# Where the Strassen weight sums of an MLP are issued: ACT and GpSimd during the front, or GpSimd alone during front, merge and MLP

## The chip, the cores and the metric

The kernel runs on one core of a Trainium2 chip. The metric is device time in microseconds from launch to the last output; lower is better. The kernel before took 915.79 us (median of three runs, 911.35 to 919.47).

## What is computed

One layer of a hybrid encoder over 528 tokens (16 learned ones and 512 of the input), width 1024:

```python
u = rmsnorm(h, norm_mix)
proj = u @ w_in                                  # RWKV features, FoX features, gates
y_rw = rwkv7_branch(proj[..., :C_RW], ...)       # 8 heads, delta rule over the sequence
y_fx = fox_branch(proj[..., C_RW:C_RW + C_FX], ...)  # 8 heads, forgetting attention
merged = sig(g_A) * (y_rw @ w_out_rw) + sig(g_B) * (y_fx @ w_out_fx)
h = h + merged @ w_o
z = rmsnorm(h, norm_mlp)
h = h + square(relu(z @ w_up)) @ w_down          # 1024 -> 4096 -> 1024
```

Everything is float32. Large products are made in three passes of a split of each operand into a high and a low part.

## The kernel before

The program has three stages.

**The front** (`tile_trunk_kernel`, lines 271 to 1033). u is held in SBUF as a high and a low part. 24 projection blocks feed the recurrent heads and the attention heads, 16 more make the gates, which go to DRAM (`gd`). Several streams (the chain over chunks, the recurrent pairs, attention, FoX features, weight sums, projections) are written as generators, and `Turns.run` (line 166) lets them take turns: a stream gives back the time at which it wants to go on, and a small planner, `Clock`, keeps a model time. The order of TensorE's instructions is the order in which the streams emit them; the other engines' order is made by a scheduler. Weights are loaded by SyncE in halves of 128x512 (256 KB, tile `wraw`, four buffers), cast to the high part by ACT (`whi`) and subtracted to the low part (`wlo`), in the front by GpSimd (line 450), elsewhere by VectorE (line 237).

**The merge** (lines 1048 to 1134). Eight blocks m: two halves of `w_out`, two gates read back from DRAM (`gl0`, `gl1`, two buffers each), tanh on ACT, 24 matmuls, two multiplications on VectorE (line 1068), one addition of the two branches on GpSimd (line 1070), then `mhi` (ACT, 1071) and `mlo` (VectorE, 1072). Early up weights are loaded and split in between (1084 to 1090). Then the product with `w_o`, its first half from `load_w` (1094), its second from eight loads into `wohi` and `wolo` (1099 to 1102), the residual, the norm and the transposes to `zhi` and `zlo`.

**MLP** (lines 1138 to 1288). The hidden width is cut into three slices of 4, 6 and 6 pairs of 256 columns (`SLICES`). In each slice the up product makes a pair's squared relu `R` out of two blocks, and `left_factors` makes seven left factors of it; then seven products per pair (a Strassen-Winograd form of the down product) run against seven right factors. Three of these are quarters of `w_down`; four are sums of quarters, T1 to T4, held in DRAM as `tsum`, in eight pieces of 256x512 (512 KB) each, one for two pairs. A product's weights are loaded as they are needed, two ahead.

**The weight sums** (lines 1001 to 1026) are made by DMA from DRAM to DRAM. For each of the eight pieces there are four copies and four additions (`accum_op=add`):

```python
t1 = b11; t1 += b12      t3 = b12; t3 += b22
t2 = b22; t2 += t1       t4 = b21; t4 += t2
```

That is 64 transfers. The stream `weight_sums` emits them at rank -1, the n-th at model time 45 + 6 n us: copies go to ACT's queue, additions to GpSimd's, each tied behind the last instruction of its engine so that the scheduler cannot move it ahead. A copy is emitted two steps ahead of its addition. All 64 are issued in the front.

Of the kernel before, what the change touches and what calls it, by code (L numbers as in the profile page):

```python
# [9 lines left out]
F32 = mybir.dt.float32  # L10
# [4 lines left out]
ALU = mybir.AluOpType  # L15
# [12 lines left out]
CDEC = math.exp(-0.5)  # L28
SLICES = (4, 6, 6)
FIRST = (0, 4, 10)  # L30


C_MU = 0
# [155 lines left out]
def kernel(ctx, tc, ht, x, win, par, cst, gain, lora, wout, wo, wup, wdn, out, dbg=None):  # L189
    nc = tc.nc  # L190
# [76 lines left out]
    gates_d = [dr.tile([128, S], F32, name=f"gd{i}") for i in range(16)]  # L267
    quarters = [[wdn[i][256 * c:256 * c + 256] for c in range(8)] for i in range(4)]
    tsum = [[dr.tile([256, 512], F32, name=f"tsum{i}") for c in range(8)] for i in range(4)]

    with ExitStack() as st:
        up = st.enter_context(tc.tile_pool(name="up", bufs=1))
# [726 lines left out]
        turns.add(2, attention())  # L999
        turns.add(3, fox_features())  # L1000
        def weight_sums():

            def part(t, c):
                return t[c].rearrange("(a b) c -> a (b c)", b=2)

            def behind(dma, engine):
                x = next(x for x in reversed(nc.cur_bb.bb.instructions) if str(x.engine).endswith(engine) and x.name != dma.ins.name)
                tc.add_manual_dep(dma.ins, x.name, mybir.DependencyInfo(mybir.DependencyClass.NoSync, mybir.DependencyReason.DATA),
                                  reason="spread over the front")

            t1, t2, t3, t4 = tsum
            b11, b12, b22, b21 = quarters
            steps = []
            for c in range(8):
                for a, b in (((t1, b11), (t1, b12)), ((t3, b12), (t3, b22)), ((t2, b22), (t2, t1)), ((t4, b21), (t4, t2))):
                    steps += [(*a, c, False), (*b, c, True)]
            for n in range(1, len(steps) - 2, 2):
                steps[n], steps[n + 1] = steps[n + 1], steps[n]
            for n, (dst, src, c, adds) in enumerate(steps):
                yield lambda: 45.0 + 6.0 * n  # L1020
                if adds:
                    behind(nc.gpsimd.dma_start(part(dst, c), part(src, c), accum_op=ALU.add, max_dma_last_dim=2048), "Pool")
                else:
                    behind(nc.scalar.dma_start(part(dst, c), part(src, c), max_dma_last_dim=2048), "Activation")

        turns.add(-1, weight_sums())
        turns.add(8, projections(24 + 16))
# [20 lines left out]
    with ExitStack() as st:  # L1048
        mp = st.enter_context(tc.tile_pool(name="mp", bufs=1))
        for j, src in enumerate((y_rw, y_fx)):  # L1050
            for k in range(4):
                split(yhi[:, 4 * j + k, :], ylo[:, 4 * j + k, :], src[:, k, :])
        mhi = mp.tile([128, KB, S], F32R, name="mhi")
        mlo = mp.tile([128, KB, S], F32R, name="mlo")
        for m in range(KB):
            w = load_w(wout[m])
            pp = []
            for br in range(2):
                g = mp.tile([128, S], F32, name=f"gl{br}", bufs=2)
                nc.sync.dma_start(g, gates_d[8 * br + m])  # L1060
                act(g, g, AF.Tanh, scale=0.5)
                po = ppo()
                n = 0
                for k in range(4 * br, 4 * br + 4):
                    for a, b in passes(wk(w, k), (yhi, ylo)):
                        mm(po, a, b[:, k, :], start=n == 0, stop=n == 11)  # L1066
                        n += 1
                V.scalar_tensor_tensor(g, g, 1.0, po, ALU.add, ALU.mult)
                pp.append(g)
            G.tensor_tensor(pp[0], pp[0], pp[1], ALU.add)  # L1070
            merged = act(mhi[:, m, :], pp[0], AF.Copy, scale=0.5)
            V.scalar_tensor_tensor(mlo[:, m, :], pp[0], 0.5, mhi[:, m, :].bitcast(F32), ALU.mult, ALU.subtract)
        M = (mhi, mlo)
        wohi = mp.tile([128, KB, 512], F32R, name="wohi")
        wolo = mp.tile([128, KB, 512], F32R, name="wolo")
        gB = mp.tile([128, 1024], F32, name="gB2")
        nc.sync.dma_start(gB, gain.to_broadcast([128, 1024]))
        for i in range(4):
            nc.sync.dma_start(hres[:, i, :], x[128 * i:128 * i + 128, :])
        zhi = hp.tile([128, KB, S], F32R, name="zhi", tag="zhi")  # L1080
        zlo = hp.tile([128, KB, S], F32R, name="zlo", tag="zlo")
        pin = pinned(merged)
        early = []
        for j in range(2):
            we = yp.tile([128, 2, 2, 512], F32R, name=f"we{j}", tag=("y_rw", "y_fx")[j])
            for x in range(2):
                raw = wp.tile([128, 512], F32, name="wraw", bufs=4)
                nc.sync.dma_start(raw, wup[j][:, 512 * x:512 * x + 512])
                split(we[:, x, 0, :], we[:, x, 1, :], raw)
            early.append([(we[:, x, 0, :], we[:, x, 1, :]) for x in range(2)])  # L1090

        pd = [ppo() for i in range(4)]
        for b2 in range(4):
            w = load_w(wo[0, b2])
            for i, b1 in [(i, b1) for b1 in range(2) for i in range(4)] if b2 < 3 else [(i, b1) for i in range(4) for b1 in range(2)]:
                k = 2 * b2 + b1
                for n, (a, b) in enumerate(passes(M, w[b1])):
                    mm(pd[i], a[:, k, 128 * i:128 * i + 128], b, start=k == 0 and n == 0, stop=k == 7 and n == 2)
        for k in range(KB):
            raw = wp.tile([128, 512], F32, name="wraw", bufs=4)  # L1100
            nc.sync.dma_start(raw, wo[1, k // 2][:, 512 * (k % 2):512 * (k % 2) + 512])
            split(wohi[:, k, :], wolo[:, k, :], raw)
        ssb = mp.tile([128, 4], F32, name="ssb")
        for i in range(4):
            hr = hres[:, i, :512]
            V.tensor_tensor(hr, hr, pd[i], ALU.add)
            xt = mp.tile([128, 1024], F32, name="xt2", bufs=2)
            act(xt[:, :512], hr, AF.Square, accum_out=ssb[:, i:i + 1])
            V.tensor_scalar(ssb[:, i:i + 1], ssb[:, i:i + 1], 1.0 / 1024, 1e-6, ALU.mult, ALU.add)
        for i in range(4):  # L1110
            po = ppo()
            n = 0
            for k in range(KB):
                for a, b in passes(M, (wohi, wolo)):
                    mm(po, a[:, k, 128 * i:128 * i + 128], b[:, k, :], start=n == 0, stop=n == 23)  # L1115
                    n += 1
            hr = hres[:, i, :]
            V.tensor_tensor(hr[:, 512:], hr[:, 512:], po, ALU.add)
            xt = mp.tile([128, 1024], F32, name="xt2", bufs=2)
            ss = mp.tile([128, 1], F32, name="ss2", bufs=2)  # L1120
            act(xt[:, 512:], hr[:, 512:], AF.Square, accum_out=ss)
            a_ = act(ss, ss, AF.Ln, bias=ssb[:, i:i + 1], scale=1.0 / 1024)
            after(a_, pin)
            act(ss, ss, AF.Exp, scale=-0.5)
            tk = slice(128 * i, 128 * i + 128)
            for j in range(2):
                cols, kk = slice(512 * j, 512 * j + 512), slice(4 * j, 4 * j + 4)
                V.scalar_tensor_tensor(xt[:, cols], hr[:, cols], ss, gB[:, cols], ALU.mult, ALU.mult)
                pt = ppd().rearrange("p (b c) -> p b c", c=128)
                for k in range(4):  # L1130
                    nc.tensor.transpose(pt[:, k, :], xt[:, 512 * j + 128 * k:512 * j + 128 * k + 128], ident)
                A.copy(zhi[:, kk, tk], pt)
                V.tensor_tensor(zlo[:, kk, tk], pt, zhi[:, kk, tk].bitcast(F32), ALU.subtract)
        dump("hres", hres.rearrange("p a b -> p (a b)"))
# [3 lines left out]
    with ExitStack() as st:  # L1138
# [43 lines left out]
        x6, x7 = ([ppd() for i in range(2)] for _ in range(2))  # L1182

        later = []

        def soon(*jobs):
            later.extend(jobs)

        for p0, n_pairs in zip(FIRST, SLICES):
# [10 lines left out]
            for n, b_ in enumerate(blocks):  # L1200
                if held:
                    w, po = held.pop(0)
                    up_part(w, po, 256, 512)
                else:
                    w = load_w(wup[b_])
                    po = ppo()
                    up_part(w, po, 0, 512)
                if n == 2 * n_pairs - 1:
                    fill(AHEAD)
                if n % 2 == 0:  # L1210
                    R = yp.tile([128, 8, 256], F32, name="R", tag=("y_rw", "y_fx")[n // 2 % 2])
                    up_evac(po, R[:, 0:8:7, :])
                else:
                    up_evac(po, R[:, 1:3, :])
                    left_factors(fhi, flo, n // 2, R)

            first, last = p0 == 0, p0 + n_pairs == 16
# [148 lines left out]
```

## Time and profile before

| | |
|---|---|
| median of three runs | 915.79 us |
| profiled execution | 918.31 us, span 916.5 us |
| TensorE busy | 860.8 us (94%) |
| VectorE, ACT, GpSimd busy | 601.1, 464.6, 187.7 us |
| mean DMA rate | 141 GB/s, 129.46 MB in 69772 packets |
| weight load of the front | 256 KB, 3.2 us from issue to landing |
| copy of a sum (ACT's queue) | 512 KB, 4.4 us |
| addition of a sum (GpSimd's queue) | 512 KB, 7.4 us from `w_down`, 6.7 us from another sum |

A row of the table of windows gives the length of a stretch, the busy time of TensorE, its weight loads, VectorE, ACT and GpSimd (with the count of instructions), the granted TensorE clock, the busy share of the 16 DMA engines and GB/s. A row of the chain of waits gives start, length, engine and what was done or waited for; the chain is followed back from the last instruction. A row of the time line gives start, length, engine, line, operation, and in brackets the idle time of the engine just before it with what ended it. A row of waits gives who waited for whom: total us, times, longest. In the list of DMA issues stand the queue, the count, the size and the median time to landing. Register, branch and DMA-issuing instructions are not counted as busy.

### The profile page before, as it was taken

The page shows a single profiled execution, that of the slowest core. Times are in us where ns is not written, and L with a number is a line of the kernel's source. Part 1 is how long each engine was busy: PE and PEld are TensorE (multiplying, and loading weights), DVE is VectorE, ACT ScalarE, POOL GpSimd, SP SyncE. Part 2 cuts the span into 40 slices and gives each one's busy share as a digit, 9 for nine tenths or more (in the row PEclk, how much of TensorE's full clock was granted, in tenths as well). Part 3 has the DMA queues.
Part 4 walks back from the last instruction along what each step waited for, and adds up shares of the span by engine and source line. Part 5 has one row for each costly group of instructions (what it writes and reads, how often), then busy time and mean ns, then how long its engine had stood idle before and what let it go on. Part 6 is the DMA issues. An engine that isn't in the chain of part 4 may idle for free.

```text
span 916.5 us, 15714 instructions
## 1 busy us (share of the span) xinstructions
PE 860.8 (94%) x5868; PEld 699.9 (76%) x5868; DVE 601.1 (66%) x1174; ACT 464.6 (51%) x939; POOL 187.7 (20%) x177
## 2 busy tenths in 40 slices
PE   6589897999989899999999999999999999999998
PEld 4587785867887777767867877888888888888886
DVE  7966875555877697465366756467556675566776
ACT  7756342585545443467364645245544454344542
POOL 4253533314533345222401210000000000000000
PEclk9889988999989899999997999999999999999999
DMA  6122634748464546665686644024632356422465
GB/s 209 46 71 70 161 94 136 185 105 209 105 140 117 138 133 188 174 161 138 152 218 218 213 164 128 1 79 131 193 126 93 104 178 194 156 96 101 137 222 170
DMA packets 69772, 129.46 MB, mean 141 GB/s; under 512 B 6840, under 2 KB 7992, under 8 KB 69696
## 3 DMA queue, kind: packets, MB, share of 16 engines
q1 hardware_dynamic: 52288, 94.91, 32.0%
q0 software_dynamic: 8704, 16.78, 11.4%
q10 hardware_dynamic: 8704, 16.78, 5.5%
q8 instruction: 46, 0.75, 0.3%
q14 instruction: 30, 0.25, 0.1%
HBM read 122.13 MB, written 39.86 MB: 177 GB/s over the span
## 4 chain that ended last, share of the span: by engine, by line
PE 72%; DVE 16%; DMA 4%; ACT 4%; issue 3%; POOL 0%; POOLq 0%; SPq 0%; ACTq 0%; DVEq 0%
PE po L1145 19%; PE pj L478 17%; PE po L1235 12%; PE pd L1235 5%; PE po L1066 2%; PE po L1115 2%; DMA wraw<-in_win 2%; PE pw L830 2%; PE py L627 1%; PE psc L582 1%; DVE tmp L812 1%; DVE AX L824 1%; PE pbt L778 1%; DVE xt L379 1%; PE psr L763 1%
## 5 line engine op out<-in xcount | busy, mean ns | idle before, releaser
L237 DVE TENSOR_TENSOR wlo<-wraw,whi 128x512 fp32r<-128x512 f32 x196 | 138.3, 713 | 95.4 <-ACT whi L236 95.3
L236 ACT CAST whi<-wraw 128x512 fp32r<-128x512 f32 x200 | 123.7, 621 | 134.8 <-PE po L1145 43.9
L478 PE MATMUL pj<-uhi,whi 128*128 128x264 f32 (+1 forms) x480 | 170.9, 356 | 10.4 <-ACT gt L489 4.7
L478 PE MATMUL pj<-uhi,wlo 128*128 128x264 f32 (+1 forms) x480 | 158.5, 330 | 0.0
L478 PE MATMUL pj<-ulo,whi 128*128 128x264 f32 (+1 forms) x480 | 158.4, 330 | 0.0
L450 POOL TENSOR_TENSOR wlo<-wraw,whi 128x512 fp32r<-128x512 f32 x80 | 110.3, 1389 | 173.9 <-ACT whi L449 155.4
L478 PEld LDWEIGHTS pj<-uhi,whi 128*128 128x128 f32 x480 | 94.3, 197 | 31.9 <-issue 11.6
L478 PEld LDWEIGHTS pj<-uhi,wlo 128*128 128x128 f32 x480 | 94.7, 197 | 7.2
L478 PEld LDWEIGHTS pj<-ulo,whi 128*128 128x128 f32 x480 | 95.0, 198 | 4.2
L1145 PE MATMUL po<-zhi,whi 128*128 128x512 f32 (+1 forms) x248 | 94.8, 382 | 0.0
L1145 PE MATMUL po<-zlo,whi 128*128 128x512 f32 (+1 forms) x248 | 94.8, 382 | 0.0
L1145 PE MATMUL po<-zhi,wlo 128*128 128x512 f32 (+1 forms) x248 | 94.8, 382 | 0.0
L449 ACT CAST whi<-wraw 128x512 fp32r<-128x512 f32 x80 | 49.4, 618 | 52.4 <-PE pj L478 29.8
L1235 PE MATMUL po<-wlo,fhi 128*128 128x512 f32 x160 | 62.3, 390 | 0.0
L1235 PE MATMUL po<-whi,flo 128*128 128x512 f32 x160 | 62.3, 390 | 0.0
L1235 PE MATMUL po<-whi,fhi 128*128 128x512 f32 x160 | 62.2, 389 | 0.0
L1145 PEld LDWEIGHTS po<-zlo,whi 128*128 128x128 f32 x248 | 46.6, 188 | 9.1
L1145 PEld LDWEIGHTS po<-zhi,wlo 128*128 128x128 f32 x248 | 46.6, 188 | 9.0
L1145 PEld LDWEIGHTS po<-zhi,whi 128*128 128x128 f32 x248 | 46.6, 188 | 9.0
L1157 ACT CAST fhi<-R 128x768 fp32r<-128x768 f32 (+1 forms) x32 | 30.2, 944 | 24.2 <-DVE R L1164 13.6
L1158 DVE TENSOR_TENSOR flo<-R,fhi 128x768 fp32r<-128x768 f32 (+1 forms) x32 | 34.8, 1088 | 7.8 <-ACT fhi L1157 7.8
L1235 PEld LDWEIGHTS po<-wlo,fhi 128*128 128x128 f32 x160 | 30.0, 188 | 6.5 <-DVE wlo L237 0.2
(295 smaller groups left out, 1667.9 us busy)
## 6 DMA issues: line engine op xcount, KB each, us to landing
wraw<-in_win SPq DMA_DIRECT2D x84, 256.0 KB, 3.2
tsum<-in_wdn ACTq DMA_DIRECT2D x32, 512.0 KB, 4.4
wraw<-in_wup SPq DMA_DIRECT2D x64, 256.0 KB, 2.6
wraw<-tsum SPq DMA_DIRECT2D x64, 256.0 KB, 2.8
wraw<-in_wdn SPq DMA_DIRECT2D x48, 256.0 KB, 2.6
tsum<-in_wdn POOLq DMA_DIRECT2D x16, 512.0 KB, 7.4
tsum<-tsum POOLq DMA_DIRECT2D x16, 512.0 KB, 6.7
gd<-gt SPq DMA_DIRECT2D x16, 256.0 KB, 2.4
```

Of the source, the lines that this page charges most:

```text
L236: A.copy(hi, raw)
L237: low.tensor_tensor(lo, raw, hi.bitcast(F32), ALU.subtract)
L449: A.copy(hi, raw)
L450: G.tensor_tensor(lo, raw, hi.bitcast(F32), ALU.subtract)
L478: mm(po, a, b[:, k, a0:a1], start=n == 0, stop=n == 23)
L830: mm(ps_[hs, n - b0, :], lhs(n)[hs], rhs(n)[hs], start=True, stop=True)
L1066: mm(po, a, b[:, k, :], start=n == 0, stop=n == 11)
L1115: mm(po, a[:, k, 128 * i:128 * i + 128], b[:, k, :], start=n == 0, stop=n == 23)
L1145: mm(po[:, t0:t1], a, b[:, k, t0:t1], start=n == 0, stop=n == 23)
L1157: A.copy(fhi[:, j, a:b], R[:, a:b])
L1158: V.tensor_tensor(flo[:, j, a:b], R[:, a:b], fhi[:, j, a:b].bitcast(F32), ALU.subtract)
L1235: mm(x[i], a[:, k, left, 128 * i:128 * i + 128], c, start=start and k == 0 and n == 0, stop=stop and k == n_pairs - 1 and n == 2)
```

## The change

A class `Sums`, made ahead of the front, holds the 64 steps in a new order, and `step()` issues the next one. All go to GpSimd's queue, each behind the last GpSimd instruction emitted so far. The order runs in rounds: first the four copies of piece 0, then for each piece its four additions, each followed by one copy of the next piece. So a copy stands eight steps ahead of its addition, and an addition that reads another sum two or more steps behind the addition that makes it. The order within a round is T1, T3, T2, T4.

The steps are issued at three places: 28 (`HEAD`) in the front, from model time 50 us on, 13.6 us apart; eight in the merge, one ahead of each block m; and 28 in MLP, four after every second up block while there are any left (seven times: four in the first slice, three in the second). In MLP a copy of one column of the fresh `R` into a new tile `pace` on GpSimd goes ahead of the four, so that they wait for that block. ACT issues no sums any more.

```diff
+HEAD = 28
+    class Sums:
+        def __init__(self):
+            t1, t2, t3, t4 = tsum
+            b11, b12, b22, b21 = quarters
+            rounds = []
+            for c in range(8):
+                rounds.append([(t[c], b[c], False) for t, b in ((t1, b11), (t3, b12), (t2, b22), (t4, b21))])
+                rounds.append([(t[c], b[c], True) for t, b in ((t1, b12), (t3, b22), (t2, t1), (t4, t2))])
+            self.steps = rounds[0]
+            for a, b in zip(rounds[1::2], rounds[2::2] + [[]]):
+                for n in range(4):
+                    self.steps += a[n:n + 1] + b[n:n + 1]
+        def step(self):
+            if not self.steps:
+                return
+            dst, src, adds = self.steps.pop(0)
+            dst, src = (t.rearrange("(a b) c -> a (b c)", b=2) for t in (dst, src))
+            prev = next((x for x in reversed(nc.cur_bb.bb.instructions) if str(x.engine).endswith("Pool")), None)
+            dma = G.dma_start(dst, src, max_dma_last_dim=2048, **({"accum_op": ALU.add} if adds else {}))
+            if prev is not None:
+                tc.add_manual_dep(dma.ins, prev.name, ...)
+    sums = Sums()
...
         def weight_sums():
-            for n, (dst, src, c, adds) in enumerate(steps):
-                yield lambda: 45.0 + 6.0 * n
-                if adds:
-                    behind(nc.gpsimd.dma_start(part(dst, c), part(src, c), accum_op=ALU.add, max_dma_last_dim=2048), "Pool")
-                else:
-                    behind(nc.scalar.dma_start(part(dst, c), part(src, c), max_dma_last_dim=2048), "Activation")
+            for n in range(HEAD):
+                yield lambda: 50.0 + 380.0 / HEAD * n
+                sums.step()
...
         for m in range(KB):
+            sums.step()
             w = load_w(wout[m])
...
+        pace = dp.tile([128, 1], F32, name="pace")
...
                     up_evac(po, R[:, 1:3, :])
+                    if sums.steps:
+                        G.tensor_copy(pace, R[:, 2, :1])
+                        for _ in range(4):
+                            sums.step()
                     left_factors(fhi, flo, n // 2, R)
```

More of the change, by code (lines that the diff above doesn't have):

```diff
@@ L269 @@
     tsum = [[dr.tile([256, 512], F32, name=f"tsum{i}") for c in range(8)] for i in range(4)]
+    class Sums:
[18 more added lines that the diff above has]
+            if prev is not None:
+                tc.add_manual_dep(dma.ins, prev.name, mybir.DependencyInfo(mybir.DependencyClass.NoSync, mybir.DependencyReason.DATA),
+                                  reason="spread over the kernel")
+    sums = Sums()
     with ExitStack() as st:
@@ L1001, in weight_sums @@
         def weight_sums():
[L1003 to L1018, printed above, removed]
-            for n, (dst, src, c, adds) in enumerate(steps):
-                yield lambda: 45.0 + 6.0 * n
-                if adds:
-                    behind(nc.gpsimd.dma_start(part(dst, c), part(src, c), accum_op=ALU.add, max_dma_last_dim=2048), "Pool")
-                else:
-                    behind(nc.scalar.dma_start(part(dst, c), part(src, c), max_dma_last_dim=2048), "Activation")
+            for n in range(HEAD):
+                yield lambda: 50.0 + 380.0 / HEAD * n
+                sums.step()
         turns.add(-1, weight_sums())
```

## Prediction

> **What bounds the kernel now.** I read the page first (span, queues, chain), then a table of windows by stage, then the chain of waits and the time line around the stages that the change touches.
>
> ```profile
> span 916.5 us, 15714 instructions
> PE 72%; DVE 16%; DMA 4%; ACT 4%; issue 3%; POOL 0%; POOLq 0%; SPq 0%; ACTq 0%; DVEq 0%
> q1 hardware_dynamic: 52288, 94.91, 32.0%
> q0 software_dynamic: 8704, 16.78, 11.4%
> q10 hardware_dynamic: 8704, 16.78, 5.5%
> ```
>
> TensorE carries 72% of the chain, GpSimd and the queues that issue the sums nearly nothing. q0 holds the 32 additions, q10 the 32 copies, q1 all that SyncE loads and stores.
>
> ```profile
> 499.00:538.00 39.00, 38.71 (x170) 31.45 (x169) 29.90 (x40) 21.18 (x37) 9.30 (x7) 1.00 0.65 206
> 583.50:629.00 45.50, 45.39 (x273) 40.52 (x272) 25.30 (x38) 18.34 (x30) 0.00 (x0) 1.00 0.20 60
> 629.00:667.00 38.00, 38.00 (x169) 31.32 (x168) 24.82 (x38) 21.67 (x35) 0.00 (x0) 1.00 0.60 185
> 667.00:733.00 66.00, 66.00 (x293) 54.66 (x292) 41.46 (x63) 29.90 (x47) 0.00 (x0) 1.00 0.31 104
> 153.50:160.40 6.90, 5.75 (x35) 3.86 (x36) 1.18 (x7) 3.02 (x6) 3.16 (x3) 0.51 0.55 193
> 307.10:314.00 6.90, 6.90 (x38) 6.00 (x40) 2.27 (x5) 3.28 (x5) 2.18 (x2) 0.51 0.77 218
> 340.00:350.00 10.00, 8.70 (x52) 7.57 (x51) 9.77 (x15) 2.92 (x7) 5.01 (x4) 1.00 0.71 230
> ```
>
> Columns: length, then busy time of PE, PEld, DVE, ACT and POOL, the granted clock, the DMA share, GB/s. The merge (499 to 538) has PE full and the DMA engines already 0.65 busy. MLP (from 583.5) is pure TensorE: nothing there can become faster, only slower. The last three rows are stretches of the front, two of them at half clock. What comes ahead of those stretches:
>
> ```profile
> 154.66 0.79 PE L478 MATMUL pj<-uhi,whi 128*128 128x512 f32 x1 [4.69 <-ACT gt L489]
> 307.05 2.26 PE L763 MATMUL psr<-L,BK 64*128 64x128 f32 x12 [2.32 <-DVE BK L722]
> 344.86 0.50 PE L478 MATMUL pj<-uhi,whi 128*128 128x512 f32 x1 [1.30 <-ACT vf L541]
> 229.54 0.45 PE L895 MATMUL pch<-Rs,Tt 64*64 64x64 f32 x8 [0.69 <-DVE Rs L891]
> 557.94 0.50 PE L1115 MATMUL po<-wohi,mhi 128*128 128x512 f32 x1 [0.89 <-DVE hres L1106]
> ```
>
> PE idle of 4.69 and of 2.32 us is followed by 6.9 us at half clock, 1.30 us is not (clock 1.00 around 345). Half clock for 6.9 us costs about 3.4 us of matmul time. So an idle stretch of over 2 us costs itself and 3.4 us more.
>
> **The change, part by part.** PE's instructions keep their order, as built; what follows is about the other queues.
>
> *ACT loses 32 issues.*
>
> ```profile
> L1024 ACTq DMA_DIRECT2D tsum<-in_wdn x32: 497/497/588, 85.8 to 468.2; - x32
> L1022 POOL DMA_DIRECT2D tsum<-in_wdn x16: 859/882/1202, 94.9 to 456.3; - x16
> 153.51 0.50 ACTq L1024
> 423.26 0.50 ACTq L1024
> 149.79 3.50 DMA wraw<-in_win
> 219.58 8.08 DMA wraw<-in_win
> POOL tsum L1022 <- DMA tsum<-in_wdn: 35.0, 6, 9.1
> 120.97 0.95 POOL L791 MEMSET AX<- 128x1024 f32 x1 [11.91 <-PE pbt L778]
> ```
>
> 32 x 0.497 = 15.9 us leave ACT, but on the chain of waits such an issue stands twice, 0.50 us each: I take -1.0 us (bounds 0 and -15.9).
>
> *GpSimd has 28 issues in the front in place of 32* (0.88 us each): -3.5 us of an engine that has 0% of the chain: 0. Copies are now eight steps ahead of their additions, so most of the 35.0 us in six waits goes; none of them stands on the chain: 0 as well. In the built order one new wait comes: the first addition to t3 stands right behind its own copy, with the memset of AX behind it. That memset had 11.91 us of idle ahead of it, which covers a wait of 9.1 us, the longest now; without the cover it would hold the inverse by that much.
>
> *Sums in the front fall from 64 to 28.* One weight load on the chain took 8.08 us with an addition and a copy in flight; it ended only 0.69 us of PE idle (229.54), so I take -0.7 (bounds 0 and -5). The two half-clock stretches quoted lie behind waits for a gate's eviction and for DVE's BK, with no load of more than 3.50 us (149.79) on their chain; what is late next there is the same. Front: -1.7 us.
>
> *Eight steps in the merge.* Step m stands on GpSimd directly behind the gl addition of block m-1 and ahead of that of block m; the first stands ahead of all gl additions and can go before 490. So from 499 to 538 come 7: four copies, three additions.
>
> ```profile
> 508.20 1.29 POOL L1070 TENSOR_TENSOR gl<-gl,gl 128x512 f32<-128x512 f32 x1 [4.31 <-DVE gl L1068]
> SPq L1060 <- POOL gl L1070: 16.7, 6, 6.5
> 516.64 3.23 DMA gl<-gd
> 523.76 3.58 DMA wraw<-in_wup
> 529.35 3.89 DMA gl<-gd
> 557.29 0.61 DVE hres L1106
> 538.78 0.63 ACT L1071 ACTIVATE mhi<-gl 128x512 fp32r<-128x512 f32 x1 [3.27 <-POOL gl L1070]
> 540.72 1.14 ACT L236 CAST whi<-wraw 128x512 fp32r<-128x512 f32 x2
> 732.54 24.48 PE po L1235 x108
> ```
>
> The issue itself (0.88) fits into GpSimd's idle ahead of gl (4.31): 0, and the waits in these steps are for transfers two or more steps old. The bytes are another matter. An addition keeps the 16 engines 0.114 x 916.5 / 32 = 3.27 us, a copy 0.055 x 916.5 / 32 = 1.58. That is 3 x 3.27 + 4 x 1.58 = 16.1 us more in a window in which they are busy 0.65 x 39 = 25.4: 41.5 us of work in 39. SyncE's loads get late, and in this stage loads are on the chain: gl, the early wup weights, gl again. They come round as a loop: a gl buffer is free when block m's mlo is made, its load must be back for block m+2; and SyncE's queue holds all later loads behind gl's wait for GpSimd (16.7 us). The price of one leg: the front between 200 and 260 us has eleven sums in 60 us, the density of seven in 39.
>
> ```profile
> wraw<-in_win SPq DMA_DIRECT2D x11, 256.0 KB, 4.0
> tsum<-in_wdn ACTq DMA_DIRECT2D x5, 512.0 KB, 4.4
> tsum<-in_wdn POOLq DMA_DIRECT2D x4, 512.0 KB, 8.7
> tsum<-tsum POOLq DMA_DIRECT2D x2, 512.0 KB, 8.7
> ...
> wraw<-in_wup SPq DMA_DIRECT2D x16, 256.0 KB, 2.5
> ```
>
> There a load of 256 KB takes 4.0 us (median), 2.5 in MLP (670 to 730) with no sums: +1.5. The worst, 8.08 us, is +4.5 over these legs. I take the middle, +3.0 a leg, 9.0 for three. Of that 2.7 us is absorbed once, since a gate of branch 0 is needed for DVE's order only when branch 1's product ends, half a block later (12 matmuls x 24.48/108). So mhi of the last block, at 538.78 now, comes 6.3 us later, and ACT has the casts of w_o (540.72) behind it, they free the buffers for the last loads of w_o, and PE waits for those at 557.94, where it waits 0.89 us now. 6.3 us of idle, and half clock behind it, 3.4: +9.7 us. Bounds: 0, if all is absorbed (a gain is excluded: only transfers are added), and 13.5 + 3.4 = 16.9, three legs at 8.08.
>
> The Trainium skill ("TensorE: Matmul & The Clock Gate", "Part 1: The HAM clock gate") has the clock halve only after a whole idle window of about 3.4 us. The trace differs: 2.32 us was enough at 307. By that rule, idle that comes in pieces under 3.4 us would leave the clock alone; the sum would then be 3.4 us less. That is the second rival below.
>
> *28 steps in MLP, in groups of four.* The small pace copy and the issues run on GpSimd, idle there; DVE's write of R now waits for the pace copy two pairs back (4 blocks of 24 x 24.48/108 = 5.4 us): 0. Groups 1 to 3 fall into the first slice's up stage: two additions and two copies are 9.7 us, 29.1 + 0.20 x 45.5 = 38.2 of 45.5. Group 4 starts with the first products: 9.7 + 0.60 x 38 = 32.5 of 38. The rest (9.7 x 2 + 4 x 3.27 = 32.5) + 0.31 x 66 = 53 of 66. All fit, unlike the merge, and up weights are loaded two blocks (10.9 us) ahead. I take 0. If the cover fails it is at 630 to 646, where a product needs a load each 6 x 24.48/108 = 1.36 us: two additions could hold it by two legs of +2 and a clock step, bound +8.
>
> *The sum*, against the profiled execution (918.31, of which the span is 916.5): 918.3 - 1.7 + 9.7 + 0 = 926.3. The median of the three runs, 915.79, lies 2.5 under that execution, so for a median I forecast 924 (923.8).
>
> **The rivals.** (1) The merge absorbs the delay: against it, 41.5 in 39 and a chain that already ends in PE idle; for it, PE idles only 0.3 us of the 39. 918.3 - 1.7 = 916.6, median 914. (2) The loads are late, but PE's idle comes in pieces and the clock stays: 926.3 - 3.4 = 922.9, median 920. For it: the 1.30 us row. (3) Faster: the front's idle is made by late loads that hold ACT and DVE in their order, more than the chain tells; with 28 sums two of its half-clock stretches vanish, 2 x (2.3 to 4.7 + 3.4), about 13 us. Against it: no sum was on their chain. 926.3 - 13 = 913.3, median 911; it decides for faster once the front returns more than the 9.7. (4) MLP products starve at 630: 926.3 + 8 = 934, median 932.
>
> **How the numbers follow.** Forecast 0.34 (its own range 919 to 930), rivals in order 0.18, 0.18, 0.16, 0.14. One percent of 915.8 is 9.2, about what a measurement of this kernel can tell from no change. Over 925: rival 4 and two fifths of the forecast, 0.14 + 0.14, and 0.08 for the merge at its upper bound out of the others: 0.36. Under 906.6: most of rival 3 if the merge also costs less than I take: 0.11. Within: 0.53. Low 908 leaves out a tenth (rival 3 with an absorbed merge), high 934 the merge's bound together with MLP's.
>
> **What would show it.** Right: gl and wraw loads between 499 and 538 with a median of 5 us or more, DMA share there near 0.9, PE idle of over 2 us near 557 with PEclk 0.5 behind it, the start of MLP some 8 us later, MLP's length unchanged, the front's end at most 3 us earlier. Wrong: gl loads at 3 us as now; a front that ends over 5 us earlier; PE idle inside MLP.

## The result and the profile after

| | before | after |
|---|---|---|
| median | 916.24 us (4 runs, 911.35 to 919.47) | 929.94 us (4 runs, 928.35 to 934.35) |
| profiled execution | 918.31, span 916.5 | 928.35, span 926.6 |

The ratio is 1.0142, 95% interval 1.0106 to 1.0178: slower by 1.1 to 1.8%, or 13.0 us (9.7 to 16.3). The forecast was 924, its range 908 to 934. The page of the kernel after, its span, the queue of the sums and its chain:

```profile
span 926.6 us, 15730 instructions
...
q0 software_dynamic: 13312, 33.56, 15.7%
...
PE 73%; DVE 14%; DMA 6%; ACT 3%; issue 2%; POOL 0%; SPq 0%; ACTq 0%; DVEq 0%; POOLq 0%
```

DMA has gone from 4% of the chain to 6%. The sums on one queue take 15.7% of the engines' time, less than the 11.4 + 5.5 of before. Next is the table of windows for the same stretches as before (merge, the start of w_o's product, the first slice's products, the second slice's up stage). They are moved by about the shift of their stage, except for the first products, which are read in the same place as before (moved by their 2.4 us, TensorE is busy the same 36.63 us). The third row is the stretch at half clock within the second. A row ends with granted clock, DMA share and GB/s.

```profile
491.00:530.00 39.00, 37.85 (x164) 30.19 (x163) 25.88 (x34) 18.39 (x32) 11.61 (x13) 1.00 0.82 240
530.00:550.00 20.00, 13.08 (x47) 10.22 (x47) 7.91 (x12) 7.82 (x12) 3.31 (x3) 0.74 0.56 178
532.40:542.60 10.20, 4.92 (x12) 3.82 (x13) 4.28 (x7) 4.15 (x7) 1.59 (x1) 0.50 0.59 212
629.00:667.00 38.00, 36.63 (x148) 27.07 (x148) 21.92 (x34) 17.57 (x29) 3.47 (x5) 1.00 0.92 272
669.50:735.50 66.00, 66.00 (x293) 54.51 (x292) 42.15 (x64) 31.09 (x48) 11.17 (x15) 1.00 0.78 203
```

TensorE is no longer full in two of them: 6.9 us are missing from the 20 after 530, with the clock at 0.50 for 10.2 us, of which 5.3 lie in the idle itself; and 1.4 from the first slice's products, 148 matmuls beginning there instead of 169. The second slice's up stage is untouched, at a DMA share of 0.78.

Where the idle of the first place stands, on the time line of TensorE, and what ends last there, on the chain of waits of the kernel after:

```profile
528.65 0.47 PE L1108 MATMUL po<-whi,mhi 128*128 128x512 f32 x1 [0.87 <-issue]
...
537.68 0.80 PE L1108 MATMUL po<-whi,mhi 128*128 128x512 f32 x1 [6.92 <-DVE gl L1078]
```

```profile
493.12 4.50 DMA gl<-gd
...
499.61 5.08 DMA gl<-gd
...
509.90 2.66 DMA gl<-gd
...
515.54 6.94 DMA wraw<-in_wup
...
527.98 7.10 DMA gl<-gd
...
536.95 0.69 DVE gl L1078
```

What VectorE and ACT did there, from their time lines, and the window of the load of 7.10 us:

```profile
536.95 0.68 DVE L1078 SCALAR_TENSOR_TENSOR gl<-gl,po 128x512 f32<-128x512 f32 x1
540.60 0.64 ACT L1081 ACTIVATE mhi<-gl 128x512 fp32r<-128x512 f32 x1 [3.26 <-POOL gl L1080]
```

```profile
528.00:535.10 7.10, 2.03 (x6) 0.97 (x6) 2.44 (x4) 1.25 (x2) 1.83 (x2) 0.81 1.07 306
```

The list of DMA issues of the kernel after, from 491 to 530, gives the medians of the merge's loads:

```profile
gl<-gd SPq DMA_DIRECT2D x12, 256.0 KB, 4.5
...
wraw<-in_wout SPq DMA_DIRECT2D x8, 256.0 KB, 4.8
```

Before they were 2.9 and 3.1. One idle stretch of 6.92 us, ahead of the seventh matmul of w_o's product, waits for the last block's gate: its load was issued at 527.98 and took 7.10 us, the up weight load ahead of it 6.94. Before, these two legs took 3.89 and 3.58. While the load of 7.10 us ran, the DMA engines were full (1.07).

Why this matmul needs that gate can be read from the kernel. It begins the third of the four output blocks of w_o's first half. Merge and w_o take turns on the same four accumulators of TensorE (PSUM buffers, `ppo()`), and the third block gets the one that still holds branch 0's product of the last merge block. VectorE frees it when it multiplies that product with its gate (line 1078), at 536.95 + 0.69 us, and TensorE goes on 0.04 us later. In e1, e5 and e9 (below) the same matmul starts 0.04 us behind the same multiplication. It is not a wait for the last block's `mhi`, which is made only at 540.60.

**Where the time went, stage by stage.** TensorE executes the same instructions in the same order in all kernels here, so the start of the n-th can be compared. The table gives start minus start in the profiled execution of the kernel before, in us, at six points of the latter; the step from one column to the next is what a stage costs. It includes the experiments. A row is one execution (e8's is the fastest of its twelve, e1's and e5's lie 8 and 6 us over their medians), so the steps say more than the totals.

| kernel | front's end 489 | w_o 545 | MLP 600 | first products' end 665 | slice 2's end 790 | last products 910 |
|---|---|---|---|---|---|---|
| after | -7.6 | 3.6 | 2.4 | 7.1 | 8.9 | 10.4 |
| e1_pace_elsewhere | -2.2 | 8.7 | 7.4 | 16.4 | 16.4 | 16.9 |
| e2_before_with_pace | 0.8 | 1.7 | 1.6 | 2.5 | 4.3 | 5.8 |
| e3_none_in_merge | -2.6 | -3.2 | -3.3 | 2.9 | 4.7 | 6.2 |
| e4_merge_steps_later | -5.2 | -5.5 | -5.4 | -0.5 | 1.3 | 2.9 |
| e5_clear_of_products | -0.4 | 12.3 | 11.1 | 12.1 | 13.8 | 15.4 |
| e6_front64_gpsimd | 7.7 | 6.0 | 5.1 | 5.0 | 5.0 | 5.6 |
| e7_all_three | -3.2 | -2.8 | -3.2 | -3.3 | -2.6 | -2.0 |
| e8_all_three_act | -11.2 | -12.5 | -12.5 | -12.6 | -11.7 | -11.8 |
| e9_half_in_merge | -0.1 | 5.4 | 4.2 | 9.1 | 10.9 | 12.6 |
| e10_before_pace_64B | -1.2 | -0.8 | -1.1 | -0.1 | 1.7 | 4.2 |
| e11_before_all_32B_up | -2.8 | -2.3 | -2.1 | -2.1 | -2.1 | -1.1 |
| e12_front_16 | -7.2 | -7.9 | -7.9 | -8.0 | -7.3 | -6.6 |

For the changed kernel: the front gives 7.6 in this execution, the way from there into w_o's product costs 11.2, of which 1.2 come back before MLP, the first slice's products cost 4.7 and the products of slices 2 and 3 another 3.3. The last item is in no term of the prediction, and the front differs by up to 7 us between executions of the same code (after, e1, e4 and e5 have one front), so each item was tested by itself.

### The profile page after: what moved, and what is told of

Its sections match the earlier page's. It is cut to its first block, busy times and chain, and to the rows that moved or that the text cites. A ratio compares the mean times of both kernels' runs of the same rounds, so it can differ in the third digit from the quotient of the medians.

```text
span 926.6 us, 15730 instructions
## 1 busy us (share of the span) xinstructions
PE 864.5 (93%) x5868; PEld 696.1 (75%) x5868; DVE 600.3 (65%) x1174; ACT 464.8 (50%) x939; POOL 209.5 (23%) x216
## 3 DMA queue, kind: packets, MB, share of 16 engines
q0 software_dynamic: 13312, 33.56, 15.7%
## 4 chain that ended last, share of the span: by engine, by line
PE 73%; DVE 14%; DMA 6%; ACT 3%; issue 2%; POOL 0%; SPq 0%; ACTq 0%; DVEq 0%; POOLq 0%
PE pj L507 19%; PE po L1155 19%; PE po L1250 11%; PE pd L1250 4%; PE po L1108 2%; PE po L1125 2%; DMA gl<-gd 2%; PE pw L859 1%; DMA wraw<-tsum 1%; PE py L656 1%; DVE tmp L841 1%; PE psc L611 1%; DVE xt L408 1%; DVE L L761 1%; PE pbt L807 1%
## 5 line engine op out<-in xcount | busy, mean ns | idle before, releaser
L507 PE MATMUL pj<-uhi,whi 128*128 128x264 f32 (+1 forms) x480 | 169.6, 353 | 11.2 <-DVE orr L336 4.6
L479 POOL TENSOR_TENSOR wlo<-wraw,whi 128x512 fp32r<-128x512 f32 x80 | 108.3, 1361 | 206.2 <-ACT whi L478 191.5
L293 POOL DMA_DIRECT2D tsum<-in_wdn x48 | 36.3, 925 | 6.2 <-DMA tsum<-in_wdn 4.3
```

The lines of the kernel that those rows point to most:

```text
L293: dma = G.dma_start(dst, src, max_dma_last_dim=2048, **({"accum_op": ALU.add} if adds else {}))
L479: G.tensor_tensor(lo, raw, hi.bitcast(F32), ALU.subtract)
L507: mm(po, a, b[:, k, a0:a1], start=n == 0, stop=n == 23)
```

## The experiments

Each was timed against the kernel before on the same chip, and the ratios are to that; there the kernel before took 918.6 to 920.8 us, so a time that an expectation gives for a chip where it takes 916 is 3 to 5 us higher here.

**A 4-byte tile.** In MLP the product matmuls themselves had become slower. These are rows of the groups of instructions, shapes kept apart (least/median/longest ns), of the kernel before and of the kernel after:

```profile
L1235 PE MATMUL po<-whi,fhi x160: 388/389/393, 628.9 to 911.3; 128*128 128x512 f32 x160
L1235 PE MATMUL pd<-whi,fhi x64: 389/389/389, 645.3 to 894.9; 128*128 128x512 f32 x64
```

```profile
L1250 PE MATMUL po<-whi,fhi x160: 388/395/501, 631.3 to 921.8; 128*128 128x512 f32 x160
L1250 PE MATMUL pd<-whi,fhi x64: 395/396/501, 650.4 to 905.0; 128*128 128x512 f32 x64
```

Six to seven ns more on each of 672 matmuls (the rows show 224, the others give 396), through all three slices, even where no sum runs. Besides the sums there was one candidate: the new tile `pace` of 4 bytes, allocated ahead of `fhi`, lifts `fhi` from address 131040 to 131072 in the compiled program, and `flo` and `r` likewise by 32 bytes.

```diff
# e1_pace_elsewhere (the kernel after with)
-        pace = dp.tile([128, 1], F32, name="pace")
-                        G.tensor_copy(pace, R[:, 2, :1])
+                        G.tensor_copy(qg8, R[:, 2, :1])
# e2_before_with_pace (the kernel before with)
+        pace = dp.tile([128, 1], F32, name="pace")
+                    if p0 + n // 2 < 7:
+                        G.tensor_copy(pace, R[:, 2, :1])
```

> The changed kernel, except that the seven 4-byte copies that pace the MLP's groups of sums write into an old constant tile (qg8) instead of a new 4-byte tile; without the new tile fhi, flo and r lie 32 bytes lower in SBUF, as in the kernel before. Theory (the 32 bytes cost the products): the 672 product matmuls start 227 ns apart at the median again instead of 232 to 235, the drift of 0.3 us per 10 us in the products of slices 2 and 3 is gone, and the time falls by about 4 us to 926. Rival (the products are slowed by the DMA load of the moved sums or by weights that come late): spacing and time as in the changed kernel, 930.

> The kernel before, with only the new 4-byte tile and seven 4-byte GpSimd copies into it; all sums stay in the front. Theory (32 bytes of address): product matmuls 232 to 235 ns apart and about 4 us more than before, 920. Rival (DMA load of the moved sums): 227 ns and 916, no change.

The rows of e1_pace_elsewhere and of e2_before_with_pace:

```profile
L1249 PE MATMUL po<-whi,fhi x160: 388/389/507, 636.4 to 928.2; 128*128 128x512 f32 x160
```

```profile
L1238 PE MATMUL po<-whi,fhi x160: 392/395/396, 630.5 to 917.2; 128*128 128x512 f32 x160
L1238 PE MATMUL pd<-whi,fhi x64: 395/396/396, 647.3 to 900.4; 128*128 128x512 f32 x64
```

The tile alone makes the kernel before slow in the products, and without it, with the same small copies, the changed kernel is at 389 again. The traces of all 14 kernels divide so: 394 to 396 ns in the seven with a new tile ahead of `fhi`, 389 in the seven without. From start to start the medians are 227 ns (e1) and 232 to 235 (e2). In the table e2 loses 4.2 us from MLP's start to its end; its ratio is 1.0024 (0.9998 to 1.0051). e1 came to 1.0073 (1.0042 to 1.0103), more of a gain on 1.0142 than the 4 us expected; the front's scatter is part of both numbers.

Two single executions asked what about the address matters.

```diff
# e10_before_pace_64B (e2 with)
-        pace = dp.tile([128, 1], F32, name="pace")
+        pace = dp.tile([128, 16], F32, name="pace")
# e11_before_all_32B_up (the kernel before with)
+    pad = cp.tile([128, 1], F32, name="pad")
+    V.memset(pad, 0.0)
     cs = cp.tile([128, 576], F32, name="cs")
```

> As e2_before_with_pace, with a new tile of 64 bytes instead of 4, so that fhi and flo lie 64 bytes higher than in the kernel before (address 32 modulo 64 again) instead of 32 (0 modulo 64). Theory 1 (what counts is the address modulo 64): product matmuls 227 ns apart as before. Theory 2 (what counts is something else that the new tile does, or any shift): 232 to 235 ns.

> The kernel before with one unused 4-byte tile (a memset on DVE) ahead of all others, which lifts every SBUF tile by 32 bytes, fhi and flo to 131072 as in the changed kernel. Theory 1a (left and right factor must lie alike modulo 64): all matmuls as before, products 227 ns apart, time unchanged. Theory 1b (a left factor at 0 modulo 64 is loaded slower, wherever the other lies): products at 232 to 235 ns, the up products, whose left factor moves too, likewise, and some 10 us or more over the whole.

The rows of e10 and of e11:

```profile
L1238 PE MATMUL po<-whi,fhi x160: 391/394/399, 627.9 to 915.6; 128*128 128x512 f32 x160
```

```profile
L1237 PE MATMUL po<-whi,fhi x160: 388/389/397, 626.8 to 910.2; 128*128 128x512 f32 x160
```

With everything lifted by 32 bytes, `fhi` again at 131072, the products stay at 389: the absolute address does not count. With `fhi` 64 bytes up they are at 394: the address modulo 64 does not count either. What is left is how the moved tiles (`fhi`, `flo`, `r`) lie to the others; the likeliest pair are the two operands of the product, the left factor and the right factor `whi`. In the compiled programs both begin at the same address modulo 512 in the kernel before (480) and in e11 (0), and at different ones in the kernel after (0 against 480) and e10 (32 against 480). That these two must agree, and modulo what, fits four cases and is not shown further.

**The merge.** Two kernels without its eight sums, and one with four.

```diff
# e3_none_in_merge; e9_half_in_merge has HEAD = 32 and "if m % 2 == 0:" ahead of the step
-HEAD = 28
+HEAD = 36
         for m in range(KB):
-            sums.step()
# e4_merge_steps_later: the steps out of the merge, HEAD unchanged, and behind the loop over wohi
+        G.tensor_copy(qg8, wolo[:, KB - 1, :1].bitcast(F32))
+        for _ in range(8):
+            sums.step()
```

> The changed kernel without the eight steps in the merge: HEAD is 36, so the front takes 36 sums and the MLP the same 28. Theory (the merge's late loads cost about 10 us): the merge's 32 loads fall back to 2.5 to 3 us, the TensorE idle before the w_o product and the half-clock stretch behind it go, the merge is about 10 us shorter, and the front stays within 2 us of the changed kernel's: 919 to 921. Rival (the 10 us are the front's gain given back at a place that would wait anyway, the loads only being late by as much as the front is early): the merge stays within 3 us of the changed kernel's, 927 to 930.

> The changed kernel with the merge's eight sums issued in a row by GpSimd after the last load of wo's second half has been converted (a 4-byte copy from its lower part paces them), so about 566 to 600, where the DMA engines are idle; the front's 28 and the MLP's 28 stay. Theory (only the collision with the merge's loads costs): about 10 us less than the changed kernel, 919 to 921, the norm's part unchanged. Rival (moved sums cost wherever they run): 925 to 930, the loss turning up between 566 and 630.

> The changed kernel with four sums in the merge instead of eight (one for every other group; the front takes 32, the MLP 28). Theory (the merge's DMA engines are overfull: 16.1 us of sums on 25.4 busy in 39): four sums leave them at about 33.5 of 39 us, so the merge costs 0 to 3 us instead of 10.5. Rival (each sum delays the load issued behind it by its own time, at whatever load): half the cost, 5 us or more.

The ratios are 1.0044 (1.0022 to 1.0066), 1.0025 (0.9994 to 1.0057) and 1.0106 (1.0064 to 1.0148). In the table e3 and e4 lose nothing between the front's end and MLP (-0.7 and -0.2), where the kernel after, e1 and e5 lose 10.0, 9.6 and 11.5. The same eight transfers of e4 run from 552 to 577 instead and cost nothing there: windows of e4, its merge and the stretch with the sums.

```profile
483.00:522.00 39.00, 38.65 (x173) 31.78 (x170) 26.91 (x37) 21.61 (x37) 8.57 (x6) 0.95 0.66 211
552.00:590.00 38.00, 37.28 (x220) 32.14 (x221) 18.47 (x31) 13.63 (x35) 5.75 (x8) 1.00 0.59 148
```

So it is the collision with the merge's loads, not the sums as such. But e9 was to show that the DMA engines must be overfull over the stage for it, and it shows the contrary. Its windows, and TensorE's time line:

```profile
491.00:535.00 44.00, 44.00 (x194) 35.86 (x192) 27.45 (x39) 22.16 (x38) 11.46 (x10) 1.00 0.78 247
535.00:555.00 20.00, 15.12 (x60) 12.08 (x59) 9.25 (x15) 10.01 (x16) 2.23 (x2) 0.83 0.44 135
```

```profile
540.11 0.79 PE L1109 MATMUL po<-whi,mhi 128*128 128x512 f32 x1 [4.88 <-DVE gl L1079]
```

With four sums the engines are 0.78 busy, and the merge still costs 4.3 us net (5.5 up to w_o): an idle of 4.88 us at the same instruction, its chain ending in `gl<-gd` from 532.44, 5.06 us long, with a single sum (529.27 to 535.63) in flight beside it. That load was issued 0.9 us ahead of w_o's first matmul (0.7 in the kernel after, 4.9 before), so most of this idle comes from the loads ahead of it, which were late already. The rival is nearer: sums lengthen the loads beside them at a mean share of 0.78 too. By the ratio alone, 1.0106 against 1.0142, e9 and the kernel after can't be told apart.

The wait needs both the late gate and the shared accumulators. In the program four more of these (`ppd()`) have no use until the norm's transposes; whether w_o's first half in those would hide the late gate was not tried.

**The first slice's products.** The chain of waits of the kernel after at the start of the products, with its third and fourth group of sums in flight, and the window of the first of its two loads:

```profile
637.75 8.10 DMA wraw<-tsum
...
647.32 5.59 DMA wraw<-tsum
...
656.20 7.03 PE pd L1250 x29
```

```profile
637.70:645.90 8.20, 7.74 (x31) 5.33 (x30) 3.23 (x5) 2.98 (x5) 1.45 (x2) 1.00 1.04 326
```

How far ahead a load is issued can be read from the kernel before: the n-th load belongs to the n-th six matmuls. Here is one load's issue, and the first of its matmuls, 7.9 us later:

```profile
645.56 0.32 SPq L233 DMA_DIRECT2D wraw<-tsum  x1
653.50 0.39 PE L1235 MATMUL pd<-whi,fhi 128*128 128x512 f32 x1
```

For the loads of `tsum` in that slice it is 6.4 to 7.9 us. In the second slice's up stage it is 8 us for the first load and 17 from the eighth on.

```diff
# e5_clear_of_products (the kernel after with)
-                    if sums.steps:
+                    if sums.steps and (p0 > 0 or n < 4):
-                        for _ in range(4):
+                        for _ in range(4 if p0 == 0 else 5):
```

> The changed kernel with the same 28 sums in the MLP, but two groups of four in the first slice's up stage (after its second and fourth block) and four groups of five in the second slice's, so that no sum runs when the first slice's products begin. Theory (the first slice's products wait for weight loads that share the DMA engines with the third and fourth group): the 256 KB loads under 630 to 660 fall from 6 to 8 us to about 3, the 4 to 9 us that the traces show lost there go, and the time is 5 to 6 us under the changed kernel, 924. Rival (the same collision only moves to the start of the second slice's products, near 730): 929 to 932, the loss turning up there.

The windows of e5, the same first products and the following up stage:

```profile
638.70:676.70 38.00, 38.00 (x165) 30.62 (x164) 23.54 (x36) 20.33 (x34) 0.00 (x0) 1.00 0.63 180
676.70:742.70 66.00, 66.00 (x293) 54.60 (x292) 42.36 (x65) 30.55 (x47) 15.30 (x22) 1.00 0.88 238
```

TensorE is full again, 165 matmuls begin in place of 148, and the step from MLP's start to 665 is 1.0 us instead of 4.7, what the 4-byte tile costs there (0.9 in e2). The twenty sums that now stand in the second slice's up stage (twelve before) cost nothing at a DMA share of 0.88, nor does the start of that slice's products. The ratio, 1.0100 (1.0062 to 1.0137), lies in the direction expected, but its interval overlaps that of the kernel after; the stage's own step is the evidence. With the groups left in place the same stage cost 6.2 (e3), 4.9 (e4), 4.9 (e9) and 9.0 us (e1). In e1 the waits ended in idle in which the clock dropped, in its time line and its window:

```profile
661.40 0.79 PE L1249 MATMUL pd<-whi,fhi 128*128 128x512 f32 x1 [2.85 <-ACT whi L237]
```

```profile
661.40:668.20 6.80, 6.80 (x17) 5.07 (x18) 4.69 (x8) 2.99 (x5) 0.00 (x0) 0.56 0.57 161
```

**The front, and all together.** e6 has the front's edit without its thinning (HEAD = 64, `pace` moved as in e1). e7 takes e1, e4 and e5 together. e8 gives e7's front copies back to ACT, and e12 thins e7's front further.

```diff
# e8_all_three_act, in Sums.step, called with True in the front
+            on_act = act_copies and not adds
-            dma = G.dma_start(...)
+            dma = (A if on_act else G).dma_start(...)
# e12_front_16 (e7 with)
-HEAD = 28
+HEAD = 16
-                    if sums.steps and (p0 > 0 or n < 4):
+                    if sums.steps and n < (4 if p0 == 0 else 8):
```

> All 64 sums in the front as before, 5.9 us apart, but all issued by GpSimd in the changed kernel's order, with nothing in merge and MLP and no new tile: the front's edit without its thinning. Theory 1 (the front gains because fewer sums run beside it): no gain, 0 to 2 us either way of the kernel before, 914 to 918 on a chip where that takes 916. Theory 2 (the front gains because ACT loses 32 issues or by the new order): 4 to 6 us faster than before, like the changed kernel's front.

> The changed kernel with the three costs taken out together: the pacing copies write to an old tile, the merge's eight sums are issued behind the last converted load of wo's second half, and the MLP's 28 come as two groups of four in the first slice and four of five in the second. Theory: the costs add, 3.6 + 10.6 + 5 off the changed kernel, so 5 us faster than the kernel before, about 911 where that takes 916. Rival (they overlap or move on): level with the kernel before or slower.

> As e7_all_three, but the copies among the front's 28 sums (20 of them) are issued by ACT, as before the change. Theory 1 (thinning gains, the issuing engine doesn't matter): within 1 us of e7_all_three. Theory 2 (ACT's issues cost): 2 to 4 us slower than e7_all_three, in the front.

> As e7_all_three with 16 sums in the front instead of 28, 24 us apart; the twelve taken out come in the third slice's up stage as two groups of five and one of two. Theory (thinning the front gains, and a group in an up stage that ends well before the products is free): 2 to 3 us less than e7_all_three, about 0.994 of the kernel before. Rival (the front's gain is used up at 28, or the third slice's sums cost): level with e7_all_three or slower.

| kernel | median | ratio to before, 95% |
|---|---|---|
| e6_front64_gpsimd | 921.36 | 1.0020 (0.9993 to 1.0048) |
| e7_all_three | 914.67 | 0.9966 (0.9937 to 0.9994) |
| e8_all_three_act | 914.62 | 0.9948 (0.9920 to 0.9976) |
| e12_front_16 | 912.84 | 0.9935 (0.9907 to 0.9964) |

(16 of the front's 28 sums are copies, not 20 as the expectation of e8 says.) Freeing ACT of its issues shows no gain: all 64 on GpSimd is no faster than before, and giving 16 copies back to ACT is no slower. Both runs also move the issues to or from GpSimd, and their intervals reach some 2.6 us to each side, so 1 us is not excluded. Thinning gains, as e6 and e7, on one chip, show (921.36 and 914.67). And e7 loses no time after the front, its row of the table stays between -3.3 and -2.0, and so do the MLP windows (e7, first products):

```profile
626.00:664.00 38.00, 38.00 (x169) 31.49 (x168) 25.17 (x39) 21.36 (x35) 0.00 (x0) 1.00 0.63 186
```

169 matmuls, as before. So no loss is left beside the three costs, and what remains is the front's gain, 3 us by the ratio (0.0034 x 918.6, 0.6 to 5.8 by the interval) where 5 were expected. e12, 0.36 to 0.93% under the kernel before, has the lowest ratio of the set, but is level with e7 and e8 within the intervals. It puts twelve sums into the third slice's up stage, where they cost nothing either (-7.3 at 790, -6.6 at 910).

## Why the prediction was right, and where it was wrong

The sum was 918.3 to 926.3, 8.0 us of loss. The profiled execution took 928.35, the median (929.94) lies 6 us over the 924 forecast for it, and the measured loss is 13.0 us (9.7 to 16.3). The median lies in the range because that reaches from 908 to 934, with an upper end made for late loads in merge and MLP together. Of the signs that the prediction set for itself, two of those against it came (the front ends 7.6 us earlier, and TensorE idles inside MLP), and of those for it only some: the merge's loads were late, with a median of 4.5 to 4.8 and not 5, and idle was followed by half clock, but not near 557. The front's term was about right in size, the merge's right in size but not in its path, and MLP's was missing.

**Front, -1.7: about right in size, its parts not shown.** The five profiles with 28 sums issued by GpSimd (after, e1, e4, e5, e7) give -7.6, -2.2, -5.2, -0.4 and -3.2, mean -3.7; the four with the old front (before, e2, e10, e11) 0, 0.8, -1.2 and -2.8, mean -0.8. That makes -2.9, with a scatter that does not tell it from -1.7. The -1.0 for ACT's issues does not show (e6, e8); the gain comes with fewer sums beside the loads, for which -0.7 was put. The scatter goes with the clock. From 40 us to the front's end the records of the granted clock in the traces have 30.6 us of half clock (after), 37.4 (e4), 44.2 (e1), 44.2 (e7) and 54.4 (e5), in the order of the shifts; with the old front 37.5 in e11 and 44.3 in before, e2 and e10. So at like clock the thinner front is 2 to 3 us shorter. Windows from 100 to 200 us of the kernel after and of e1, which have the same front, show it too.

```profile
100.00:200.00 100.00, 89.05 (x928) 70.39 (x928) 67.11 (x150) 50.58 (x116) 35.45 (x36) 0.97 0.34 102
```

```profile
100.00:200.00 100.00, 89.56 (x869) 72.34 (x867) 64.73 (x143) 46.20 (x103) 34.96 (x35) 0.91 0.32 92
```

0.97 and 0.91 of full clock over 100 us are 6 us of clock, and at the front's end the two differ by 5.4. The Trainium skill ("TensorE: Matmul & The Clock Gate", "Part 1: The HAM clock gate") says that the window in which activity is counted runs freely, so that the number of slow matmuls at the start of one kernel differs from run to run. The traces agree, for the whole front: one code has 30.6 to 54.4 us of half clock there. The kernel after has 13.7 us less of it than the kernel before, which is 6.8 of the 7.6 us. Rival 3 (two half-clock stretches of the front vanish) was thus met by the execution that happened to be profiled (one stretch gone, one half as long), and not by the code: that the front ended over 5 us earlier was chance.

**Merge, +9.7: right in size and in its late loads, wrong in its path.** The table has +11.2 to w_o and 1.2 given back, +10.0 (9.6 and 11.5 in e1 and e5, nothing without the sums). Idle was to be 6.3 us and is 0.87 + 6.92 = 7.8; half clock was to cost 3.4 and costs 2.5 (4.92 us busy at 0.50). The loads came late as said (gl 4.5 us in the median, 2.9 before), and their delays added up from block to block: the last block's first gate was issued 4.2 us later against w_o's first matmul than before and took 3.2 us longer. But the prediction let that gate delay `mhi`, ACT's casts behind it and w_o's last loads near 557, where the kernel after has no wait. TensorE waited 20 us earlier, for the accumulator that the last block's first product still held. Both paths begin with the same late gate, and that the size fits is in part luck. The argument of 41.5 us of work in 39 failed as well: the engines were busy 0.82 x 39 = 32.0 us, and in e9 half the sums cost about half the time at 0.78. They were full only while the long loads ran (1.07). Rival 1 (the merge absorbs the delay) fell with that idle, and rival 2 (idle in pieces, the clock stays) too: 6.92 of the 7.8 us were one piece. In e1, 2.85 us of idle brought a stretch of 6.8 us at 0.56. The same section of the Trainium skill asks for a whole idle window of about 3.4 us. As with the 2.32 us of the prediction, the trace differs.

**MLP, 0: wrong, +8.0.** The prediction named it as what would prove it wrong: waits of TensorE inside MLP. Two things. Rival 4 took place beside the forecast: the first slice's products starved, for 3.8 us here (4.7 less 0.9 for the tile) where its bound was 8, and 9.0 in e1 once the clock dropped. The step that failed is "All fit": it compared busy times over a stage (32.5 of 38 us; 0.92 of 38, 35.0, were measured), and over the stage they did fit. They did not while the long loads ran: the share was 1.04 over the load of 8.10 us. The right test is a single load's. It is issued 6.4 to 7.9 us ahead of its first matmul (not two products, 2.7 us, as the program's "two ahead" suggests: SyncE issues it as soon as one of four `wraw` buffers is free), and the two casts take 1.4 of that. So a load of up to 5 to 6.5 us is covered, an estimate from these rows; the three loads that ran first beside the fourth group took 7.15, 7.50 and 8.10 us, and the next products came 1.75 to 2.2 us apart instead of 1.4. In the up stages loads are issued up to 17 us ahead, and there loads of 6 to 8 us cost nothing, even at 0.88 in e5. The other part, 0.9 + 3.3 us, is the 4-byte tile, which the prediction costed as a copy on GpSimd and not as an allocation.

The three together, -7.6 + 10.0 + 8.0 = 10.4, are the shift of the last products. In the profiled execution the total was close because the front's lucky clock paid for MLP. With the front at the -2.9 of the means it would be 15.1, and by the ratio it is 13.0: there the missing MLP term shows.

## What to carry to other kernels

When transfers are moved under other loads, the DMA engines' mean share over a stage doesn't decide: TensorE lost time at 0.78 (e9), 0.82 and 0.92, and none at 0.88 (e5). Look in the trace how far ahead of its use each neighbouring load is issued: 7 us of latency cost nothing where weights are issued 17 us ahead, and starved TensorE where it was 6 to 8. And ask what TensorE lacks when it waits; here it was once the weights and once a buffer that a late transfer kept from being freed. Small allocations count: after adding a tile, compare the mean duration of the matmuls whose operands moved. Before giving a stage credit in one profile, look at the clock in it, and at a second profile of the same code.

## What the runs showed that was not expected

- Shifting the left factors (with `r`) by 32 or 64 bytes against all other tiles makes a float32 matmul of 128x128 by 128x512 5 to 7 ns slower (389 to 394 or 396), or 5 to 8 from start to start; the weight load itself stays at 188 ns. Over 672 matmuls that is about 4 us (e2). Lifting all tiles alike costs nothing (e11).
- One 512 KB transfer from DRAM to DRAM is enough to be seen: beside it and some other loads, the 256 KB load of the last block's first gate took 5.06 us (e9); without it 2.71 to 4.26 (e4, before, e3).
- Half clock lasted 3.4 us or a whole multiple of it (6.8, 10.2, 13.7, 17.1) in all traces, but for the stretch that the program's end cuts off. It began 2.0 us into an idle of 2.85 (e1) and 1.6 us into one of 6.92 (after); in the first case 6.0 of its 6.8 us fell on matmuls, in the second 4.9 of 10.2.
